# The first product of a two-block kernel in six stages in place of five, and the order of its column groups

## Chip, cores and metric

The kernel runs on one core of a Trainium2 chip. The metric is the device time of one execution in microseconds (us), as the median of several. In the rows below PE is TensorE (PEld its weight loads), DVE VectorE, ACT ScalarE, POOL GpSimd, SP SyncE, which issues most of the DMAs; "Lnnn" is a line of the kernel before.

## What is computed

One sequence of 256 tokens of width 2048 goes through three layers; the change touches only the beginning of the first. Cut to that:

```python
cond = silu(c)
mod = cond @ ada_w[0] + ada_b[0]             # ada_w[0]: 2048 x 6144
shift, scale, gate = split(mod, 3)
h = rms_norm(x, pre_g[0]) * (1 + scale) + shift
u, v, z = split(h @ w_in, 3)                 # w_in: 2048 x 12288
v = layer_norm(gelu(v), norm_g)              # gelu(u), silu(z) and w_out follow
...
x = x + gate * rms_norm(y, post_g[0])
```

All of it is float32. Each product is made of rounded float32r operands: both factors are split into a high part and a rest, and three of the four partial products are added up.

## The kernel before

Everything streams from HBM through two rings of buffers: `raw`, six buffers of 512 KB, for weights and for the rows of `ada_w` that VectorE works on, and five slots of 1 MB (the `s` tiles 7 to 11) for the rows of `ada_w` that TensorE works on. `plan` (L457) writes down in what order the entries are loaded; `fill` (L178) issues them on SP in that order, with at most three entries of look-ahead past one whose ring is full. An entry is issued when the instruction that frees its buffer has been emitted, and SP then waits for that instruction.

The first product is v, 2048 input rows by 4096 columns. It can't begin with all rows at once, because the operand h needs shift and scale, which are themselves a product with 32 MB of `ada_w`. So `stages` (L819) works in stages over the input rows. `STAGES` gives their bounds in tiles of 128 rows. In stage s TensorE multiplies the stage's rows of `w_in` with the part of h that is already there, and between those pieces it makes shift and scale for the rows of stage s+1:

- a piece ("w", `product`, L955) is 256 rows by one group of 512 columns: ScalarE casts the 512 KB of `raw` to the high part `wh` (L885), VectorE subtracts for the rest `wl` (L887), and TensorE runs 12 matmuls of 512 columns (L303 to L305), six for each half of the tokens;
- `mod` (L900) runs the products with `ada_w` (L912), two entries of 1 MB at a time; `rows` (L920) copies their sum out, and `fin` (L927) turns it into columns (L934), adds the bias (L937, L940) and makes the operand's tiles, two at a time, with `h_tiles` (L609: L615 on VectorE, L616 on ScalarE, L620 on VectorE).

There are eight column groups, visited in the order of `ORDER`. Groups 6 and 7 (`STAY`) keep their sums in four PSUM banks through all stages. The other six share three banks, taken in turn by one half of the tokens at a time: at the end of each stage the sum of such a half is copied out by ScalarE (first stage, L970) or added by VectorE to a partial sum in SBUF (L972, tiles `s`, `y`, `wst`), and the bank is free for the half that comes three later. In the last stage the sums go on to a gelu on ScalarE (L765). The eighth bank (7) is that of `mod` and `fin`.

`ahead` (L868) splits weights up to three pieces ahead of the one that TensorE works on, so on VectorE the split of piece p+3 stands before the sums of piece p. It stops at pieces of a stage whose `fin` has not been emitted. When it comes to an entry of the kind "rest" (rows of `ada_w` for the gate, 512 KB each, two VectorE operations L431/L433), it emits that work too. `fin` calls `ahead` once more between its first and its second pair of operand tiles. In the last stage `biases` (L712) puts ten small loads on SP before the fifth piece.

In `plan` a stage of 8 pieces puts the entries of `mod` among its first 5 pieces, then `rows`, one piece, `fin`, and two pieces; a stage of 16 pieces has 12, `rows`, one, `fin`, three. What is left of `ada_w` is spread over the later products by `mix` (L552), at so many entries for each piece.

Of the kernel before, what the change touches and what calls it, by code (L numbers as in the profile page):

```python
# [63 lines left out]
class Entry:  # L64


    def __init__(self, kind, kt, n, loads, pad=False, key=None):
        self.kind, self.kt, self.n, self.loads, self.pad, self.key = kind, kt, n, loads, pad, key
        self.prep = self.use = self.ring = None


class Kernel:
    def __init__(self, ctx, tc, ins, out):
        self.ctx, self.tc, self.nc = ctx, tc, tc.nc
        self.i, self.out = ins, out
        self.W = 512

        self.RAW, self.LOOK, self.AHEAD = 6, 3, 3

        self.STAGES, self.ORDER, self.STAY = [0, 2, 4, 8, 12, 16], (0, 1, 6, 2, 3, 7, 4, 5), (6, 7)  # L80
        self.g = ctx.enter_context(tc.tile_pool(name="g", bufs=1))
        self.ps = ctx.enter_context(tc.tile_pool(name="ps", bufs=1, space=bass.MemoryType.PSUM))
        self.entries, self.issued, self.prepped, self.nraw = [], 0, 0, {}
        self.halves = {}
        self.ready, self.uses, self.adas = deque(), [], deque()
        self.flying, self.landed = [0] * 8, [0] * 8
        self.lanes = [deque() for _ in range(5)]
        self.nn = self.held = 0
        self.sent = set()
        self.taken = [-1] * 8  # L90
        self.banks([0, 1, 2, 3, 4], [5, 6])
# [376 lines left out]
    def plan(self):  # L468
        i = self.i
        E = self.entries  # L470
# [3 lines left out]
        def put(kind, e=None, **at):  # L474
            if e:
                at["n"] = len(E)
                E.append(e)
            self.walk.append((kind, at))

        for s in range(-1, len(self.STAGES) - 1):  # L480
            pieces = []
            if s >= 0:
                k0, k1 = self.STAGES[s:s + 2]
                for g in self.ORDER:
                    for k in range(k0, k1, 2):
                        pieces.append(("w", self.chunk(("v", g), w_in, k * P, 4096 + g * 512), dict(s=s, g=g, k=k)))
            if s + 2 == len(self.STAGES):
                extra = self.ada(0, 2, 0, None)
                for q, (kind, e, at) in enumerate(pieces):
                    if q == 4:  # L490
                        put("biases")
                    put(kind, e, **at)
                    if q >= 8 and extra:
                        put("rest", extra.pop(0))
                break
            k0, k1 = self.STAGES[s + 1:s + 3]
            n = (k1 - k0) * P
            kt = 2048 // n
            mods = []
            for r in range(0, 16, kt):  # L500
                for part in range(2):
                    e = self.chunk(None, i["ada_w"][0], r * P, part * 2048 + k0 * P, kt, n)
                    e.kind, e.ring = "ada0", [7, 8, 9, 10, 11]
                    mods.append(("mod", e, dict(s=s + 1, part=part, r=r, kt=kt)))
            done = 0
            room = max(1, len(pieces) - (3 if len(pieces) == 8 else 4))
            for q in range(room if pieces else 0):
                put(*pieces[q][:2], **pieces[q][2])
                while done < len(mods) and (done + 0.5) * room < (q + 1) * len(mods):
                    put(*mods[done][:2], **mods[done][2])  # L510
                    done += 1
            for kind, e, at in mods[done:]:
                put(kind, e, **at)
            put("rows", s=s + 1)
            for kind, e, at in pieces[room:room + 1]:
                put(kind, e, **at)
            put("fin", s=s + 1)
            for kind, e, at in pieces[room + 1:]:
                put(kind, e, **at)
        rest = []  # L520
        for s in range(1, 4):
            rest += self.ada(0, 2, s, (lambda: self.gate_done(0)) if s == 3 else None)
        for part in (0, 1):
            for s in range(4):
# [1 line left out]
        main = []  # L526
# [3 lines left out]
            main += self.group(("z", g), w_in, 8192 + g * 512, 16)  # L530
        for g in range(4):
            main += self.group(("sgu_out", g), i["sgu_w_out"][0], g * 512, 32)
        E += self.mix(main, rest, [(64, 0.7), (64, 0.2), (56, 0.58)])
        rest = []
        for s in range(4):
            rest += self.ada(1, 2, s, (lambda: self.gate_done(1)) if s == 3 else None)
        w = i["mla_w_in"][0]
        main = []
# [27 lines left out]
        w = i["w_in_2"][0]  # L566
# [280 lines left out]
    def stages(self, h, uv, v_out):  # L847
# [3 lines left out]
        walk, E = self.walk, self.entries  # L851
        n_st = len(self.STAGES) - 1
        parts, room = {}, [3, 3, 3]
# [13 lines left out]
        st = dict(at=0, ahead=0, turn=0, fin=-1)  # L867
        pair = {}  # L868

        def begin(n):  # L870
            self.fill()
            v = self.nraw.pop(n)
            self.prepped = max(self.prepped, n + 1)
            return v

        def ahead(m, mods=True):

            while st["at"] < len(walk):
                kind, at = walk[st["at"]]
                if kind == "w":  # L880
                    if st["ahead"] >= m or at["s"] > st["fin"]:
                        return
                    v = begin(at["n"])
                    hi = self.t("wh", [P, 1024], F32R, bufs=self.LOOK + 1).rearrange("p (k n) -> p k n", n=512)
                    nc.scalar.copy(hi, v)  # L885
                    lo = self.t("wl", [P, 1024], F32R, bufs=self.LOOK + 1).rearrange("p (k n) -> p k n", n=512)
                    nc.vector.tensor_tensor(out=lo, in0=v, in1=hi.bitcast(F32), op=ALU.subtract)  # L887
                    self.freed(E[at["n"]])
                    split[at["n"]] = hi, lo
                    st["ahead"] += 1  # L890
                elif kind == "mod":
                    if at["s"] > st["fin"] + 1 or not mods:
                        return
                elif kind == "rest":
                    for _ in E[at["n"]].prep(begin(at["n"])):
                        pass
                    self.freed(E[at["n"]])
                st["at"] += 1

        def mod(at):  # L900
# [13 lines left out]
                self.freed(E[m])  # L914

        def rest(at):
            if E[at["n"]].use:
                E[at["n"]].use()

        def rows(at):  # L920
            n = (self.STAGES[at["s"] + 1] - self.STAGES[at["s"]]) * P
            st["sum"] = self.t("ada", [P, 512], bufs=2)[:, 0:n]
            nc.scalar.copy(st["sum"], st["rows"][:, 0:n])
            if at["s"] == 0:
                st["fin"] = 0
                ahead(1, False)

        def fin(at):
            s = at["s"]
            k0, k1 = self.STAGES[s:s + 2]  # L930
            m = k1 - k0
            ps = self.bank(7)
            for b in range(m):
                nc.tensor.matmul(ps[:, 2 * b:2 * b + 2], st["sum"][:, b * P:b * P + P], self.halves2, start=True, stop=True)  # L934
            for part in (1, 0):
                o = part * 16 + k0
                nc.vector.tensor_tensor(out=self.mod[0][:, o:o + m], in0=ps[:, part:2 * m:2], in1=self.adab[0][:, o:o + m], op=ALU.add)  # L937
                if part:
                    a = slice(k0, k1)
                    nc.vector.scalar_tensor_tensor(out=self.a1[0][:, a], in0=self.mod[0][:, 16:32][:, a], scalar=1.0, in1=self.preg[0][:, a], op0=ALU.add, op1=ALU.mult)  # L940
            for j in range(k0, k1, 2):
                self.h_tiles(0, (j, j + 1), self.R0)
                if j == k0:
                    st["fin"] = s
                    ahead(min(3, st["ahead"] + 1), False)

        def product(at):
            s, g, k = at["s"], at["g"], at["k"]
# [27 lines left out]
                    v_out(g)(tt, four(ps))  # L976
            st["ahead"] -= 1

        do = dict(w=product, mod=mod, rows=rows, fin=fin, rest=rest, biases=lambda at: self.biases())
        self.banks([], [7])  # L980
        for p, (kind, at) in enumerate(walk):
            left = sum(1 for q in walk[p:] if q[0] == "w")
            if kind in ("w", "mod", "rest"):
                ahead(4 if kind == "w" else 3)
            if kind == "w" and left <= self.LOOK:
                while sum(1 for x in self.ready if x[0] == "piece") < self.LOOK + 1 - left:
                    self.prep_next()
                self.split_ahead(self.LOOK + 1 - left)
            do[kind](at)
# [809 lines left out]
```

## Time and profile before

| | |
|---|---|
| median of three runs | 2614.23 us (2611.59 to 2617.68) |
| the profiled execution | 2612.92 us, span 2611.0 us |
| TensorE busy | 2537.4 us, 97% of the span |
| VectorE, ScalarE busy | 1819.6 us (70%), 1393.2 us (53%) |
| mean granted TensorE clock | 0.991 |

The profile and the rows are those of one execution. The staged product takes the time from about 28 us to 265 us; before it lie the loads of x and the first products with `ada_w`, and after it the products of u, z and the rest of the three layers.

### The profile page before, as it was taken

How to read it: one execution, taken by the hardware profiler on the slowest of the kernel's cores; microseconds unless marked ns; L12 is line 12 of the kernel's file. 1: busy time of each engine (PE TensorE's matmuls, PEld its weight loads, DVE VectorE, ACT ScalarE, POOL GpSimd, SP SyncE). 2: the span in 40 equal slices, each digit the busy share in tenths (PEclk: the TensorE clock that was granted, in tenths of full speed). 3: DMA queues.
4: the chain of work that ended last, by engine and by line, in shares of the span. 5: the costliest groups of instructions: out<-in, count | busy, mean ns of one | idle time of the engine just before them, and what ended most of it. 6: DMA issues, size and time to landing. Idle time of an engine off the chain costs nothing.

```text
span 2611.0 us, 37191 instructions
## 1 busy us (share of the span) xinstructions
PE 2537.4 (97%) x14044; PEld 2166.7 (83%) x14044; DVE 1819.6 (70%) x2664; ACT 1393.2 (53%) x2116; POOL 3.0 (0%) x16
## 2 busy tenths in 40 slices
PE   7998999999998999998999999999999999999999
PEld 5666888888886888887888888888888888888887
DVE  3556898788876788866777777668665556666665
ACT  4334654455444655656566666555544545555554
POOL 0000000000000000000000000000000000000000
PEclk9999999999999999999999999999999999999999
DMA  9976898666884577654535454555556565565653
GB/s 349 355 265 213 304 319 313 208 216 205 313 282 145 179 234 228 211 170 151 160 127 166 148 161 147 191 193 186 194 187 192 188 192 186 187 193 191 195 194 128
DMA packets 302621, 546.02 MB, mean 209 GB/s; under 512 B 27370, under 2 KB 48618, under 8 KB 302058
## 3 DMA queue, kind: packets, MB, share of 16 engines
q1 hardware_dynamic: 300714, 542.71, 63.2%
q8 instruction: 110, 1.80, 0.3%
q10 hardware_dynamic: 1728, 0.94, 0.1%
q14 instruction: 69, 0.57, 0.1%
HBM read 541.48 MB, written 2.10 MB: 208 GB/s over the span
## 4 chain that ended last, share of the span: by engine, by line
PE 82%; DVE 4%; ACT 2%; DMA 2%; issue 1%; SPq 1%; ACTq 0%; DVEq 0%
PE b L295 39%; PE b L296 20%; PE b L303 6%; PE b L305 5%; PE b L304 5%; DVE wl L244 1%; DMA raw<-in_sgu_w_in 1%; ACT wh L241 1%; SPq L173 1%; DVE ada L433 1%; PE b L815 1%; DMA raw<-in_ada_w 1%; PE b L383 0%; DMA raw<-in_mla_w_ukv 0%; DVE R L390 0%
## 5 line engine op out<-in xcount | busy, mean ns | idle before, releaser
L295 PE MATMUL b<-s,wh 128*128 128x512 f32 x4800 | 1696.6, 396 | 7.6 <-DVE s L1091 5.0
L296 PE MATMUL b<-s,wl 128*128 128x256 f32 x4800 | 1344.3, 280 | 0.5 <-DVE wl L244 0.5
L241 ACT CAST wh<-raw 128x1024 fp32r<-128x1024 f32 (+2 forms) x776 | 800.6, 1039 | 859.3 <-PE b L295 563.9
L244 DVE TENSOR_TENSOR wl<-raw,wh 128x1024 fp32r<-128x1024 f32 (+2 forms) x776 | 924.9, 1210 | 249.2 <-ACT wh L241 246.5
L295 PEld LDWEIGHTS b<-s,wh 128*128 128x128 f32 x4800 | 904.1, 188 | 205.8 <-issue 5.4
L296 PEld LDWEIGHTS b<-s,wl 128*128 128x128 f32 x4800 | 904.2, 188 | 2.0 <-DVE wl L244 0.8
L303 PE MATMUL b<-wh,s 128*128 128x512 f32 x816 | 330.6, 405 | 20.3 <-DVE wst L972 11.5
L305 PE MATMUL b<-wh,s 128*128 128x512 f32 x816 | 324.6, 398 | 0.0
L304 PE MATMUL b<-wl,s 128*128 128x512 f32 x816 | 323.4, 396 | 0.0
L303 PEld LDWEIGHTS b<-wh,s 128*128 128x128 f32 x816 | 155.0, 190 | 69.8 <-DVE wst L972 13.3
L305 PEld LDWEIGHTS b<-wh,s 128*128 128x128 f32 x816 | 154.9, 190 | 39.3
L371 DVE TENSOR_TENSOR s<-s,s 128x1024 fp32r<-128x1024 f32 (+1 forms) x82 | 91.6, 1121 | 134.1 <-ACT s L370 134.1
L304 PEld LDWEIGHTS b<-wl,s 128*128 128x128 f32 x816 | 154.8, 190 | 36.1
L433 DVE SCALAR_TENSOR_TENSOR ada<-raw,cond,ada 128x512 f32<-128x512 f32 x240 | 179.6, 748 | 5.6 <-DMA raw<-in_ada_w 2.2
L316 DVE TENSOR_TENSOR cb<-b,ca 128x256 f32<-128x256 f32 x258 | 108.4, 421 | 107.6 <-ACT ca L310 104.0
L310 ACT COPY ca<-b 128x256 f32<-128x256 f32 x338 | 122.9, 368 | 45.4 <-PE b L296 34.7
L887 DVE TENSOR_TENSOR wl<-raw,wh 128x1024 fp32r<-128x1024 f32 x64 | 78.3, 1225 | 94.1 <-ACT wh L885 91.1
L885 ACT CAST wh<-raw 128x1024 fp32r<-128x1024 f32 x64 | 66.5, 1046 | 98.9 <-PE b L305 57.9
L370 ACT CAST s<-s 128x1024 fp32r<-128x1024 f32 (+1 forms) x82 | 79.0, 964 | 13.3 <-DVE s L1170 7.2
L316 DVE TENSOR_TENSOR s<-b,ca 128x256 f32<-128x256 f32 x72 | 29.7, 420 | 22.9 <-ACT ca L310 22.8
L295 PE MATMUL b<-yat,wh 128*128 128x512 f32 x128 | 44.4, 392 | 0.0
L1747 ACT ACTIVATE s<-s 128x256 f32<-128x256 f32 x64 | 26.9, 420 | 17.2 <-DVE s L1746 15.2
(324 smaller groups left out, 1520.5 us busy)
## 6 DMA issues: line engine op xcount, KB each, us to landing
raw<-in_sgu_w_in SPq DMA_DIRECT2D x192, 512.0 KB
raw<-in_w_in SPq DMA_DIRECT2D x148, 512.0 KB
raw<-in_ada_w SPq DMA_DIRECT2D x128, 512.0 KB
raw<-in_w_up SPq DMA_DIRECT2D x128, 512.0 KB
raw<-in_w_down SPq DMA_DIRECT2D x128, 512.0 KB
s<-in_ada_w SPq DMA_DIRECT2D x32, 1024.0 KB
raw<-in_sgu_w_out SPq DMA_DIRECT2D x64, 512.0 KB
raw<-in_mla_w_in SPq DMA_DIRECT2D x40, 512.0 KB
```

Source lines behind the costliest of these rows:

```text
L241: self.nc.scalar.copy(h, v[:, k0:k0 + kn, :])
L244: self.nc.vector.tensor_tensor(out=l, in0=v[:, k0:k0 + kn, :], in1=h.bitcast(F32), op=ALU.subtract)
L295: mm(ps[:, 0:512], h[:, kk, wsl], x, start=start, stop=False, skip_group_check=True)
L296: mm(ps[:, 0:256], l[:, kk, wsl], x[:, 0:256], start=False, stop=stop, skip_group_check=True)
L303: mm(ps, x[:, a:a + P], h[:, kk, wsl], start=start, stop=False, skip_group_check=True)
L304: mm(ps, x[:, a:a + P], l[:, kk, wsl], start=False, stop=False, skip_group_check=True)
L305: mm(ps, x[:, 256 + a:256 + a + P], h[:, kk, wsl], start=False, stop=stop, skip_group_check=True)
L310: self.nc.scalar.copy(c, ps[:, 256:512])
L316: self.nc.vector.tensor_tensor(out=o, in0=ps[:, 0:256], in1=c, op=ALU.add)
L370: self.nc.scalar.copy(dst[:, :, 0:256], raw)
L371: self.nc.vector.tensor_tensor(out=dst[:, :, 256:512], in0=raw, in1=dst[:, :, 0:256].bitcast(F32), op=ALU.subtract)
L433: nc.vector.scalar_tensor_tensor(out=acc[0], in0=v[:, k - k0, :], scalar=col, in1=acc[0], op0=ALU.mult, op1=ALU.add)
```

## The change

```diff
-        self.STAGES, self.ORDER, self.STAY = [0, 2, 4, 8, 12, 16], (0, 1, 6, 2, 3, 7, 4, 5), (6, 7)
+        self.STAGES, self.ORDER, self.STAY = [0, 2, 4, 6, 8, 12, 16], (0, 1, 2, 6, 3, 4, 5, 7), (6, 7)
...
             if s + 2 == len(self.STAGES):
-                extra = self.ada(0, 2, 0, None)
+                extra = (self.ada(0, 2, 0, None) + self.ada(0, 2, 1, None))
+                n_extra = 12
                 for q, (kind, e, at) in enumerate(pieces):
...
-                    if q >= 8 and extra:
+                    if q % 5 in (1, 3) and n_extra:
                         put("rest", extra.pop(0))
+                        n_extra -= 1
                 break
...
             put("fin", s=s + 1)
-            for kind, e, at in pieces[room + 1:]:
+            for kind, e, at in pieces[room + 1:room + 2]:
                 put(kind, e, **at)
-        rest = []
-        for s in range(1, 4):
+            if k1 - k0 > 2:
+                put("more", s=s + 1)
+            for kind, e, at in pieces[room + 2:]:
+                put(kind, e, **at)
+        rest = extra
+        for s in range(2, 4):
             rest += self.ada(0, 2, s, (lambda: self.gate_done(0)) if s == 3 else None)
...
-        E += self.mix(main, rest, [(64, 0.7), (64, 0.2), (56, 0.58)])
+        E += self.mix(main, rest, [(64, 0.66), (64, 0.2), (56, 0.63)])
...
-                elif kind == "rest":
-                    for _ in E[at["n"]].prep(begin(at["n"])):
-                        pass
-                    self.freed(E[at["n"]])
                 st["at"] += 1
...
         def rest(at):
+            for _ in E[at["n"]].prep(begin(at["n"])):
+                pass
+            self.freed(E[at["n"]])
             if E[at["n"]].use:
                 E[at["n"]].use()
...
-            for j in range(k0, k1, 2):
-                self.h_tiles(0, (j, j + 1), self.R0)
-                if j == k0:
-                    st["fin"] = s
-                    ahead(min(3, st["ahead"] + 1), False)
+            self.h_tiles(0, (k0, k0 + 1), self.R0)
+            st["fin"] = s
+
+        def more(at):
+            k0 = self.STAGES[at["s"]]
+            self.h_tiles(0, (k0 + 2, k0 + 3), self.R0)
```

The third stage of 512 rows becomes two of 256. In each stage the groups that stay in PSUM are now the fourth and the last, where they were the third and the sixth. `fin` makes the first pair of operand tiles, and `more`, one piece later, the second pair. The last stage has 16 pieces, of which six (q = 1, 3, 6, 8, 11, 13) are followed by an entry of the gate's rows, where before the last eight were; the others move into the products of u, z and the output.

On VectorE at the end of the last stage but one, from the second L937 of `fin` on (`cb` and `s_51` are the operand's tiles, `wl` a split of weights, `wst` a partial sum, whose `b_306` and `b_307` are the two banks of its group). Before:

```order
L937 TENSOR_TENSOR mod_7_74<-b_308_1438,cols_73 128x4
L615 SCALAR_TENSOR_TENSOR cb_1446<-x_94,a_29_124,R_188 128x256
L615 SCALAR_TENSOR_TENSOR cb_1449<-x_94,a_29_124,R_188 128x256
L620 SCALAR_TENSOR_TENSOR s_51_199<-cb_1446,mod_7_74,s_51_199 128x256
L620 SCALAR_TENSOR_TENSOR s_51_199<-cb_1449,mod_7_74,s_51_199 128x256
L615 SCALAR_TENSOR_TENSOR cb_1454<-x_94,a_29_124,R_188 128x256
L615 SCALAR_TENSOR_TENSOR cb_1457<-x_94,a_29_124,R_188 128x256
L620 SCALAR_TENSOR_TENSOR s_51_199<-cb_1454,mod_7_74,s_51_199 128x256
L620 SCALAR_TENSOR_TENSOR s_51_199<-cb_1457,mod_7_74,s_51_199 128x256
L887 TENSOR_TENSOR wl_1464<-raw_1308,wh_1462 128x1024
L972 TENSOR_TENSOR wst_206<-wst_206,b_306_1424 128x512
L972 TENSOR_TENSOR wst_206<-wst_206,b_307_1431 128x512
```

The same place in the changed kernel, whose line numbers are a few higher (L942 for L937, L621, L626 and L893 for L615, L620 and L887, L978 for L972):

```order
L942 TENSOR_TENSOR mod_7_74<-b_325_1505,cols_73 128x4
L621 SCALAR_TENSOR_TENSOR cb_1513<-x_94,a_29_124,R_188 128x256
L621 SCALAR_TENSOR_TENSOR cb_1516<-x_94,a_29_124,R_188 128x256
L626 SCALAR_TENSOR_TENSOR s_51_199<-cb_1513,mod_7_74,s_51_199 128x256
L626 SCALAR_TENSOR_TENSOR s_51_199<-cb_1516,mod_7_74,s_51_199 128x256
L893 TENSOR_TENSOR wl_1523<-raw_1373,wh_1521 128x1024
L978 TENSOR_TENSOR wst_206<-wst_206,b_323_1491 128x512
L978 TENSOR_TENSOR wst_206<-wst_206,b_324_1498 128x512
L621 SCALAR_TENSOR_TENSOR cb_1541<-x_94,a_29_124,R_188 128x256
L621 SCALAR_TENSOR_TENSOR cb_1544<-x_94,a_29_124,R_188 128x256
L626 SCALAR_TENSOR_TENSOR s_51_199<-cb_1541,mod_7_74,s_51_199 128x256
L626 SCALAR_TENSOR_TENSOR s_51_199<-cb_1544,mod_7_74,s_51_199 128x256
```

The sums of the group that is worked on around `fin` stand ahead of the second pair of operand tiles instead of behind it. That group is the seventh of the order (5) now; before it was 4, also the seventh, with group 5 still to come.

On SP in the last stage, around the end of the small loads (the `raw` from `in_sgu_w_in` are pieces, those from `in_ada_w` entries of the gate). Before:

```order
L728 DMA rows_1608<-in_k_norm 1x64 x2
L730 DMA blk_70<-in_shape_consts 128x128
L173 DMA raw_1624<-in_ada_w 128x2x512
L173 DMA raw_1642<-in_sgu_w_in 128x2x512
L173 DMA raw_1647<-in_ada_w 128x2x512
L173 DMA raw_1668<-in_sgu_w_in 128x2x512
```

In the changed kernel:

```order
L734 DMA rows_1680<-in_k_norm 1x64 x2
L736 DMA blk_70<-in_shape_consts 128x128
L173 DMA raw_1696<-in_sgu_w_in 128x2x512
L173 DMA raw_1716<-in_ada_w 128x2x512
L173 DMA raw_1738<-in_sgu_w_in 128x2x512
L173 DMA raw_1754<-in_sgu_w_in 128x2x512
```

The first load behind the small ones is a piece instead of an entry of the gate, and two pieces in four loads become three. The piece at the head is the twelfth of the stage in both kernels.

## Rows read from the trace of the kernel before

**Rows 1.** Stages 2, 4 and the sum of five: length; PE, PEld, DVE, ACT, POOL; clock, DMA, GB/s.

```profile
58.60:97.00 38.40, 33.66 (x171) 21.37 (x170) 21.32 (x31) 11.65 (x16) 0.00 (x0) 0.94 1.03 375
...
156.00:213.80 57.80, 55.54 (x265) 39.22 (x264) 30.92 (x39) 18.88 (x21) 0.00 (x0) 0.97 0.60 200
...
sum 237.64, PE 220.19 PEld 157.76 DVE 133.49 ACT 92.40 POOL 0.00; mean PE 44.04 PEld 31.55 DVE 26.70 ACT 18.48 POOL 0.00
```

**Rows 2.** Waits of PE from 27 to 266 us: us in total, times, longest.

```profile
PE b L303 <- DVE wst L972: 11.5, 4, 3.9
PE b L303 <- DVE s L972: 3.7, 2, 2.9
...
PE b L303 <- ACT s L970: 2.2, 1, 2.2
```

**Rows 3.** Timeline of PE at two waits: start, us, operation, idle before it.

```profile
147.27 0.39 PE L304 MATMUL b<-wl,s 128*128 128x512 f32 x1
147.50 0.40 PE L305 MATMUL b<-wh,s 128*128 128x512 f32 x1
150.17 0.60 PE L303 MATMUL b<-wh,s 128*128 128x512 f32 x1 [2.27 <-DVE wst L972]
...
261.00 0.50 PE L303 MATMUL b<-wh,s 128*128 128x512 f32 x1 [3.05 <-DVE wst L972]
```

**Rows 4.** Stretches behind two waits: length, PE busy, clock, DMA share, GB/s.

```profile
94.29:99.15 4.86, 4.86 (x11) 0.50 1.05 387
150.17:153.92 3.75, 3.75 (x10) 0.54 0.70 187
```

**Rows 5.** Timeline of DVE before the end of the wait of rows 3.

```profile
145.89 0.88 DVE L615 SCALAR_TENSOR_TENSOR cb<-x,a,R 128x256 f32<-128x256 f32 x2
...
148.29 1.23 DVE L887 TENSOR_TENSOR wl<-raw,wh 128x1024 fp32r<-128x1024 f32 x1 [0.45 <-ACT wh L885]
149.43 1.28 DVE L972 TENSOR_TENSOR wst<-wst,b 128x512 f32<-128x512 f32 x2
```

**Rows 6.** Timeline of DVE in the last stage.

```profile
238.69 1.54 DVE L433 SCALAR_TENSOR_TENSOR ada<-raw,cond,ada 128x512 f32<-128x512 f32 x2 [2.21 <-DMA raw<-in_ada_w]
240.14 1.28 DVE L972 TENSOR_TENSOR s<-s,b 128x512 f32<-128x512 f32 x2
...
260.26 1.28 DVE L972 TENSOR_TENSOR wst<-wst,b 128x512 f32<-128x512 f32 x2
```

**Rows 7.** Timeline of SP in the last stage: the first small load, and the load behind them.

```profile
225.44 0.42 SPq L717 DMA_DIRECT2D bs<-in_sgu_b_s  x1
...
234.35 0.40 SPq L173 DMA_DIRECT2D raw<-in_ada_w  x1
```

**Rows 8.** Timeline of PE: the products with ada_w and the columns of `fin`, short and long stage.

```profile
47.98 1.93 PE L912 MATMUL b<-s,bs 128*32 128x256 f32 x32
...
52.75 0.50 PE L934 MATMUL b<-bs,ada 128*128 128x2 f32 x4
...
137.89 1.92 PE L912 MATMUL b<-s,bs 128*32 128x512 f32 x16
...
142.64 0.95 PE L934 MATMUL b<-bs,ada 128*128 128x2 f32 x8
```

**Rows 9.** Timeline of ACT in the first two stages.

```profile
48.85 1.05 ACT L885 CAST wh<-raw 128x1024 fp32r<-128x1024 f32 x1 [2.02 <-DMA raw<-in_sgu_w_in]
...
59.76 1.07 ACT L885 CAST wh<-raw 128x1024 fp32r<-128x1024 f32 x1
66.67 1.05 ACT L885 CAST wh<-raw 128x1024 fp32r<-128x1024 f32 x1 [5.83 <-DMA raw<-in_sgu_w_in]
```

**Rows 10.** Stretches of the early loads: length, clock, DMA share, GB/s.

```profile
28.00:45.00 17.00, 0.91 1.07 367
45.00:60.00 15.00, 1.00 1.05 386
```

**Rows 11.** Stretch of PE behind the staged product, columns as in rows 4.

```profile
320.00:800.00 480.00, 479.97 (x2830) 1.00 0.79 266
```

More of the change, by code (lines that the diff above doesn't have):

```diff
@@ L977, in product @@
             st["ahead"] -= 1
-        do = dict(w=product, mod=mod, rows=rows, fin=fin, rest=rest, biases=lambda at: self.biases())
+        do = dict(w=product, mod=mod, rows=rows, fin=fin, more=more, rest=rest, biases=lambda at: self.biases())
         self.banks([], [7])
```

## The prediction

> **What bounds the kernel.** TensorE is busy 97% of the span, so I first asked in which stretch the rest is lost. Behind the staged product TensorE does not stop: 479.97 of 480 us are busy from 320 to 800 [rows 11]. In the five stages it is busy 220.2 of 237.6 us [rows 1]. The view of waits gives the idle part there: 11.5 + 3.7 + 2.2 = 17.4 us in seven waits, all before the first matmul on a PSUM bank (L303), six of them for VectorE's addition of an earlier sum out of that bank (L972) and one for ScalarE's copy (L970) [rows 2].
>
> Two more losses hang on them. Idle is counted from the modelled end of a matmul, 0.40 after its start, while the next one starts 0.23 later [rows 3]: each wait costs 0.17 more, 1.2 for seven. And behind three of the waits, those near 94, 150 and 208 us, the granted clock is 0.50 to 0.54, the lower of the two levels, 1.2 GHz [rows 4] (the third stretch, from 208.15 to 211.90, reads like the second). There 11, 9 and 9 matmuls (the shorter stretch counts the next one, which starts on its edge) take 4.86 + 3.75 + 3.75 = 12.36 us; at 0.233 each 29 take 6.76. That is 5.6 us. **All in all 17.4 + 1.2 + 5.6 = 24.2 us** can be had, no more.
>
> Why the banks are late differs by place. At the boundaries (150 us stands for 94 and 208 too) the addition that TensorE waits for starts at 149.43. Ahead of it on VectorE stand the second pair of operand tiles, from 145.89, and a split of weights at 148.29 that waited for a cast, which ScalarE does behind its part of those tiles [rows 5]. In the last stage the addition at 240.14 stands behind a gate entry whose load landed at 238.69; that load was issued at 234.35, behind ten small ones begun at 225.44 [rows 6, 7]. The addition at 260.26, for which TensorE waited 3.05 until 261.00 [rows 3], is behind eight pieces that each brought VectorE a split (1.23), a gate entry (1.54) and, for three groups in four, additions [rows 5, 6]: 1.23 + 1.54 + 0.5 = 3.3 us against 12 x 0.233 = 2.8 us of TensorE. In the first stage the copy stands behind the cast of a piece that has not landed.
>
> **The change part by part.**
>
> *Order of the groups, and the second pair later.* Three banks turn, so a half sum must be out when the third half behind it begins. Before, group 4's first half had to be out when the second half of group 5's first piece began, and `fin` with all its operand tiles lay in between. Now the group behind `fin` is one that stays and takes no bank. Group 5's two halves may wait until the next stage: with two halves of the staying group's piece in between (four in the long stages) there are at least 2.8 us more. On VectorE its additions come after one pair and one or two splits, and ahead of the second pair. Reckoned from the end of the L934 matmuls (in rows 3, 18 matmuls of 0.233 before the wait, so 147.73 - 4.2 = 143.5): the first pair is done when the second begins at 145.89 [rows 5], at about 2.5; two casts and splits until 5.5, addition until 6.1; the bank is wanted at 2 x 2.8 + 1.4 = 7.0. The second pair is wanted one piece into the next stage, at 8.4 in the tightest case, and done at about 8.2 to 8.7. So all three boundary waits go, with their clock: of the waits 11.5 less the last stage's 3.05, call it 8.5, plus 3 x 0.17 plus 5.6, is **14.6 us**. The fifth boundary, which is new, has the same slack. Bound: nothing to the whole if some split is late.
>
> *Four stages of 256 rows.* TensorE's work stays: 64 pieces, and 14 products with `ada_w` of 1.93 or 1.92 us, since 32 matmuls of 256 columns take as long as 16 of 512 [rows 8]; the L934 matmuls go with the rows and are as many. There are 12 more additions of 0.64 on VectorE, 7.7 us. They are hidden: in a short stage VectorE has 8 splits (9.8), 12 additions (7.7) and 2.5 for `fin`, 20 us beside at least 26.7 us of TensorE (22.4 + 2 x 1.95 + 0.4 for L934 [rows 8]), and it is busy 21.3 of 38.4 us now [rows 1]. Without that cover they would cost their 7.7.
>
> *Loads.* The same bytes in another order. Second stage before: 4 MB of pieces and 8 MB of `ada_w` beside 31.0 us of TensorE (22.4 + 4 x 1.95 + 0.8), with DMA at 1.03 of its share, and it took 38.4 [rows 1]. Now the second and third stages load 8.4 million bytes each in 26.7 us, 314 GB/s, under the 386 that the rows show [rows 10]. The fourth has the old second's 12.6 million bytes in 31.0 us, 406 GB/s: too fast by 0.6 million, which the two stages before it have put by, since both rings together hold over 8 million. So from 80 us on no piece is late. The wait that the old second stage had in its middle (3.7 less 2.9, so 0.8 [rows 2], and 0.17) goes: **1.0 us**.
>
> Before that, DMA still leads. First stage: the fifth group visited now begins its second bank half at 27.9 + 1.4 (slow clock at the start, kept) + 6.5 pieces, that is 5 x 2.8 + 2 x 1.95 + 1.4 = 48.6. Its bank is copied out behind the cast of the eighth piece, 48.85 to 49.9 [rows 9], and half a us of copy: 50.4. It waits 1.7, where 2.2 + 0.17 were lost: **0.7 us** gained. Second stage: its fourth piece stands behind as many bytes as before, cast at 59.76 [rows 9], but more of them are narrow rows; 28 to 45 us, with such rows, ran at 367, and 45 to 60 at 386 [rows 10], so 5.6 million bytes come 0.8 later: 60.6. Cast, split and addition end at 63.6, and the bank is wanted 4.2 after the stage's start at 57.8, at 62.0: **a new wait of 1.6 us**. Its bounds are nothing and 5.8, the longest wait of a cast for its load [rows 9].
>
> The Trainium skill, *DMA: Bandwidth & Descriptors*, Specifications, speaks against this part: it gives HBM a limit of about 358 GB/s for a core. By that the fourth stage's loads would take 35.2 us and not 31.0, and if nothing were put by the sum would come out 4.2 us higher. The trace shows 386 over 15 us, so the rows decide.
>
> *Last stage.* Six gate entries in place of eight, spread over 14 pieces, and each emitted at its place instead of three pieces early. VectorE now has 19.7 of splits, 9.2 of gate and 7.7 of additions, 36.6 us beside 44.8. The wait at 261 (3.05 + 0.17) goes. The one at 240.9 (2.91 + 0.17) shrinks. The small loads still hold SP from 11.6 to 20.5 us after the stage's start, and the twelfth piece now goes first behind them; by the 4.3 us that the old first load took [rows 6, 7] it lands at 24.8, and the thirteenth, two loads of 1.4 later, at 27.5. Its split stands ahead of the fourth group's additions: 27.5 + 1.05 + 1.25 + 0.65 = 30.4, wanted at 29.4. **Gain 3.2 + 3.1 - 1.0 = 5.3 us**; bounds 0 and 6.3.
>
> *Later products.* 0.66 entries for a piece in place of 0.7 in u, 0.63 for 0.58 in the output product; TensorE was full there, and two more gate entries are 3 us of VectorE spread over 184 pieces. Nothing; if their cover failed, 3 us.
>
> **Sum.** 14.6 + 1.0 + 0.7 - 1.6 + 5.3 = 20.0 us. The profiled execution took 2612.9 (span 2611.0 and 1.9 around it): 2592.9. The median shown is 1.3 above that execution, so I forecast 2594.2.
>
> **The rivals.**
> - *Starved in the fourth stage.* If the rings don't put by enough, because SP reaches only three entries past a full ring, that stage costs what the old second one did, 38.4 for 31.0: 7.4 us more, 2601.6. For it speaks that DMA fell to 200 GB/s at 156 to 214, with buffers full and entries stuck; against it, that no piece was late for its load there [rows 1].
> - *The last stage keeps its waits.* If the small loads hold SP longer, the stage gains nothing: 2594.2 + 5.3 = 2599.5. For it: the order of the small loads is untouched; against it: the wait at 261 was VectorE's own.
> - *Slower: a bank wait at every boundary.* Group 5's additions now stand behind splits of the next stage's pieces. If the second such piece lands more than 0.9 us after its cast could begin, TensorE stops on the second half of the next stage's first piece; five boundaries at the worst price seen, 3.9 + 0.17 + 2.3 = 6.4, are 32 us: 2626. The rate of 314 GB/s speaks against it, and the waits of casts for loads before 80 us [rows 9] for it at the first two.
> - *No change.* The waits may only move to the next bank, since three banks still turn: 2614.
>
> **Chances.** Forecast 0.73; starved 0.10; last stage 0.10; no change 0.04; slower 0.03. Low end: all 24.2 gone and a run like the fastest, 2.6 below the median: 2587. High end: both starved and no gain in the last stage, 2607. That holds over 0.8 of the cases and the bounds of the new waits. A measurement can tell about 0.2% from no change, 5.2 us, so faster means below 2609: the first three cases, 0.93, less a little for their tails: 0.91, same 0.05, slower 0.04.
>
> **What would show it.** In the new profile the waits of PE for L978 (L972's new line) fall from 15.2 to about 3 us, none of them at the five boundaries, and the clock stays at its upper level from 31 us on. The staged product ends near 245 us instead of 265. Left are a wait of 1 to 2 us near 49 and one near 62, and one about 29 us into the last stage. The prediction is wrong if waits at boundaries remain, if casts wait for loads between 85 and 200 us, or if TensorE stops in the product of u for what moved there.

## The result, and the profile after

| | before | changed |
|---|---|---|
| median, same chip | 2612.91 us (2611.5 to 2617.68, 4 runs) | 2596.12 us (2594.59 to 2597.12, 4 runs) |
| profiled span | 2611.0 | 2594.0 |
| mean granted TensorE clock | 0.991 | 0.994 |
| staged product, first L303 to first L295 | 27.86 to 265.65: 237.8 | 28.14 to 249.04: 220.9 |

The ratio is 0.9932, with an interval from 0.9915 to 0.9949: 16.8 us less, where 20.0 were forecast. The forecast of 2594.2 is 1.9 below the median. Behind the staged product both executions take the same time, 2345.3 and 2345.0 us, so all of the gain was made inside it and none was given back.

Stretches of the changed kernel, with the columns of [rows 1]: the staged product, the stretch with its two last boundaries, and the one behind its longest wait:

```profile
28.14:249.04 220.90, 215.43 (x1116) 157.10 (x1117) 139.35 (x184) 92.75 (x129) 0.00 (x0) 0.99 0.90 310
145.00:215.00 70.00, 69.57 (x330) 50.30 (x330) 44.84 (x59) 30.43 (x39) 0.00 (x0) 1.00 0.80 274
231.99:236.00 4.01, 4.01 (x11) 3.16 (x12) 2.14 (x3) 3.29 (x6) 0.00 (x0) 0.57 0.75 269
```

TensorE is idle for 5.5 of 220.9 us, where it was idle for 17.4 of 237.6. Its waits from 27 to 260 us, to be read beside [rows 2] (the one for L622 lies before the first piece and is there in both kernels):

```profile
PE b L303 <- DVE y L978: 3.0, 1, 3.0
PE b L303 <- ACT s L622: 2.9, 1, 2.9
PE b L303 <- ACT y L976: 1.2, 1, 1.2
PE b L303 <- DVE s L978: 1.2, 2, 0.9
```

The seven waits have become four, and none is at a boundary. More than half of what is left is a single wait in the last stage. The timeline of PE shows it, with the slow clock behind it (compare [rows 3, 4]):

```profile
231.99 0.49 PE L303 MATMUL b<-wh,s 128*128 128x512 f32 x1 [2.95 <-DVE y L978]
232.32 0.43 PE L304 MATMUL b<-wl,s 128*128 128x512 f32 x1
232.55 0.62 PE L305 MATMUL b<-wh,s 128*128 128x512 f32 x1
232.98 0.63 PE L303 MATMUL b<-wh,s 128*128 128x512 f32 x1
...
235.96 0.40 PE L304 MATMUL b<-wl,s 128*128 128x512 f32 x1
```

Eight matmuls from 232.55 start 0.43 apart and not 0.23, at 1.2 GHz. From start to start the last stage lost 4.7 us: 3.1 in the wait, 1.6 by the clock. What the wait hangs on is read backwards, first on DVE, then on ACT, then on SP ([rows 6, 9, 7] are their counterparts):

```profile
228.55 1.53 DVE L433 SCALAR_TENSOR_TENSOR ada<-raw,cond,ada 128x512 f32<-128x512 f32 x2
230.11 1.22 DVE L893 TENSOR_TENSOR wl<-raw,wh 128x1024 fp32r<-128x1024 f32 x1
231.25 1.28 DVE L978 TENSOR_TENSOR y<-y,b 128x512 f32<-128x512 f32 x2
```

```profile
226.32 1.05 ACT L891 CAST wh<-raw 128x1024 fp32r<-128x1024 f32 x1 [3.57 <-DMA raw<-in_sgu_w_in]
229.03 1.04 ACT L891 CAST wh<-raw 128x1024 fp32r<-128x1024 f32 x1 [1.66 <-DMA raw<-in_sgu_w_in]
```

```profile
213.55 0.42 SPq L723 DMA_DIRECT2D bs<-in_sgu_b_s  x1
...
217.10 1.54 SPq L734 DMA_DIRECT2D rows<-in_q_norm  x2
221.04 0.52 SPq L734 DMA_DIRECT2D rows<-in_k_norm  x2
221.61 0.36 SPq L736 DMA_DIRECT2D blk<-in_shape_consts  x1
222.07 0.40 SPq L173 DMA_DIRECT2D raw<-in_sgu_w_in  x1
```

The addition at 231.25 stands behind the split at 230.11, which starts when the cast from 229.03 ends, and that cast waited for a load. The gate entry at 228.55 ends as the cast ends, so it delays nothing. The late loads were issued from 222.07 on, when SP had got through the small ones (eleven with `bs` and `blk`). Among those SP waited for loads to land, as its waits from 199 to 222 us say (the first two lines, for buffers, lie ahead of the small loads):

```profile
SPq L173 <- DVE wl L893: 10.2, 6, 4.3
SPq L173 <- DVE ada L433: 4.3, 2, 2.3
SPq L734 <- DMA raw<-in_sgu_w_in: 2.5, 2, 1.4
SPq L734 <- DMA bs<-in_sgu_b_s: 2.4, 1, 2.4
```

The DMA engines were not the limit. In their rate from 212 to 232 us, in 40 slices of half a us, they stand nearly still from 219.5 to 222.5:

```profile
GB/s 315 270 352 373 242 193 295 352 385 418 434 414 353 169 117 33 50 0 0 1 1 106 91 111 299 397 389 352 377 406 406 385 410 414 385 401 381 361 381 369
```

### The profile page after: what moved, and what is told of

Same layout as the page of the kernel before. It is cut to its first block, busy times and chain, and to the rows that moved or that the text cites. A ratio compares the mean times of both kernels' runs of the same rounds, so it can differ in the third digit from the quotient of the medians.

```text
span 2594.0 us, 37345 instructions
## 1 busy us (share of the span) xinstructions
PE 2531.2 (98%) x14108; PEld 2165.2 (83%) x14108; DVE 1824.8 (70%) x2679; ACT 1390.2 (54%) x2117; POOL 3.0 (0%) x16
## 4 chain that ended last, share of the span: by engine, by line
PE 90%; DVE 3%; DMA 3%; ACT 2%; issue 1%; SPq 0%; ACTq 0%; DVEq 0%
PE b L295 42%; PE b L296 21%; PE b L303 7%; PE b L305 7%; PE b L304 7%; DMA raw<-in_sgu_w_in 2%; PE b L914 1%; PE b L821 1%; DVE wl L244 0%; DMA s<-in_ada_w 0%; ACT wh L241 0%; PE b L383 0%; SPq L173 0%; DVE R L390 0%; ACT wh L891 0%
## 5 line engine op out<-in xcount | busy, mean ns | idle before, releaser
L295 PE MATMUL b<-s,wh 128*128 128x512 f32 x4800 | 1696.1, 396 | 7.4 <-DVE s L1097 4.9
L295 PEld LDWEIGHTS b<-s,wh 128*128 128x128 f32 x4800 | 904.0, 188 | 205.2 <-issue 5.4
L303 PE MATMUL b<-wh,s 128*128 128x512 f32 x816 | 329.3, 404 | 8.3 <-DVE y L978 3.0
L303 PEld LDWEIGHTS b<-wh,s 128*128 128x128 f32 x816 | 154.0, 189 | 54.3 <-issue 5.4
L893 DVE TENSOR_TENSOR wl<-raw,wh 128x1024 fp32r<-128x1024 f32 x64 | 77.3, 1222 | 72.5 <-ACT wh L891 72.3
L295 PE MATMUL b<-yat,wh 128*128 128x512 f32 x128 | 44.4, 392 | 0.0
```

The lines of the kernel that those rows point to most:

```text
L295: mm(ps[:, 0:512], h[:, kk, wsl], x, start=start, stop=False, skip_group_check=True)
L303: mm(ps, x[:, a:a + P], h[:, kk, wsl], start=start, stop=False, skip_group_check=True)
```

## Experiments

Two questions were open: which part of the change removed the waits, and what makes the one that is left. All runs were timed beside the kernel before; its medians in the three sets were 2612.33, 2612.0 and 2613.85. The time behind the staged product differed by some us between profiled executions (2342.5 to 2348.3 over all of these kernels, 2345 to 2347 for most), so the staged product's own length is the sharper number. It differs too: two executions of the changed kernel took 220.9 and 222.0 us for it (the second is e10's), two of the kernel of e6 216.4 and 215.3 (e11). So a difference of about 1 us between single profiles proves nothing.

| run | median us | ratio to before, interval | staged product us |
|---|---|---|---|
| e5_order_alone | 2601.17 | 0.9957 [0.9943, 0.9972] | 225.7 |
| e1_old_order | 2601.74 | 0.9959 [0.9945, 0.9973] | 224.1 |
| e2_pairs_together | 2599.07 | 0.9947 [0.9932, 0.9962] | 223.0 |
| e3_old_stages | 2598.39 | 0.9947 [0.9932, 0.9962] | 223.1 |
| e4_old_gate | 2598.37 | 0.9947 [0.9930, 0.9963] | 222.4 |
| e6_small_on_pool | 2591.78 | 0.9921 [0.9906, 0.9935] | 216.4 |
| e7_no_gate_last | 2592.88 | 0.9924 [0.9909, 0.9939] | 216.1 |
| e8_pool_no_gate | 2594.30 | 0.9930 [0.9915, 0.9945] | 216.8 |
| e9_before_pool | 2611.87 | 0.9991 [0.9982, 1.0000] | 231.3 |
| e10_change_again | 2597.54 | 0.9927 [0.9914, 0.9940] | 222.0 |
| e11_pool_again | 2591.98 | 0.9908 [0.9895, 0.9922] | 215.3 |

**The order alone (e5_order_alone).** The kernel before, with one line of the change:

```diff
-... (0, 1, 6, 2, 3, 7, 4, 5), (6, 7)
+... (0, 1, 2, 6, 3, 4, 5, 7), (6, 7)
```

> The kernel before with the new order of groups alone; stages, pairs and gate weights are as before. Theory: the order removes the three boundary waits with the slow clock behind them, 14.6 us by the sum of the prediction, and leaves the last stage's 6 us of waits: 10 to 15 us faster than before, about 2600, the staged product from 237.8 us to some 223 to 228. Rival (the later second pair is needed too, since VectorE makes it ahead of the sums at the boundary): waits of 2 to 4 us stay at the boundaries of 512 rows, and no more than 6 us are gained, about 2607 to 2611.

11.2 us of the 16.8 are there, and 12.1 of the staged product's 16.9. PE's waits from 27 to 267 us, in this kernel's lines:

```profile
...
PE b L303 <- DVE y L972: 2.8, 1, 2.8
PE b L303 <- DVE s L972: 2.5, 1, 2.5
PE b L303 <- DVE wst L972: 1.9, 2, 1.1
...
```

Of the boundary waits one of 1.15 is left, near 96; none is left near 150 or 208, though both pairs of the operand are made in one go here. And the last stage has a wait of 0.8 near 243 where before lost 3.05 [rows 3], with the gate entries handled as before. So for that wait, too, the order alone is enough. The one of 2.5 at 69.77, in the second stage, was 0.8 before. The rival falls.

**The order undone (e1_old_order).** The reverse of that line, in the changed kernel.

> The changed kernel with one thing undone: the order of the groups in a stage is again 0 1 6 2 3 7 4 5, so that a stage ends on two rotating groups. Theory: the order is what removes the waits for banks at the boundaries. At each of the five boundaries the first group then wants a bank that the fifth group has just filled, and TensorE waits some 1 to 4 us for VectorE's sums; the time goes up by 4 to 14 us, about 2604, the staged product from 220.9 us to some 225 to 235, with the last stage as it is in the changed kernel. Rival: the smaller stages and the second pair made later are what frees VectorE in time, and the order alone is worth under 2 us: 2595 to 2598.

```profile
PE b L303 <- DVE wst L978: 7.6, 6, 1.7
...
```

The waits of the six groups' banks are back: 1.5 to 1.7 at each of the four places from 86 to 153 us, 0.4 near 202. Before, three such waits were 3.94, 2.27 and 2.26 long, with slow matmuls behind each; here no slow matmuls follow. By the reckoning of the prediction the boundaries cost 6.7 + 5 x 0.17 = 7.5 us in place of 14.6. So the theory holds, but the rest of the change takes off about half without the order, the slow clock with it: this kernel is 10.6 us faster than the one before. Undoing the order costs 5.6 us (3.2 of the staged product), not the 11.2 that it gives alone, so the gains of the parts overlap.

What the theory had not foreseen is the last stage: from 198 us on TensorE lost 2.1 us from start to start, in place of 4.7, and the wait in the stage's middle is not there, although the small loads end later here (at 229.34, and the stage begins 6.9 later). In the new order three groups that rotate (3, 4, 5) follow each other just where the late pieces are; in the old one a group that stays, whose bank is its own, stands among them. That is read from the order and was not tried apart.

At the stage's end the old order's wait is 0.94 here, where before lost 3.05. VectorE's work ahead of the addition for which TensorE waits is shown first as it was before (the addition is the one at 260.26 in [rows 6]), then in e1, with its wait on PE:

```profile
251.37 1.23 DVE L887 TENSOR_TENSOR wl<-raw,wh 128x1024 fp32r<-128x1024 f32 x1 [1.75 <-ACT wh L885]
252.51 1.53 DVE L433 SCALAR_TENSOR_TENSOR ada<-raw,cond,ada 128x512 f32<-128x512 f32 x2
...
255.09 1.53 DVE L433 SCALAR_TENSOR_TENSOR ada<-raw,cond,ada 128x512 f32<-128x512 f32 x2
...
257.68 1.53 DVE L433 SCALAR_TENSOR_TENSOR ada<-raw,cond,ada 128x512 f32<-128x512 f32 x2
259.13 1.22 DVE L244 TENSOR_TENSOR wl<-raw,wh 128x1024 fp32r<-128x1024 f32 x1
```

```profile
241.64 2.36 DVE L893 TENSOR_TENSOR wl<-raw,wh 128x1024 fp32r<-128x1024 f32 x2 [1.75 <-ACT wh L891]
243.92 1.53 DVE L433 SCALAR_TENSOR_TENSOR ada<-raw,cond,ada 128x512 f32<-128x512 f32 x2
...
246.50 1.22 DVE L244 TENSOR_TENSOR wl<-raw,wh 128x1024 fp32r<-128x1024 f32 x1
247.64 1.27 DVE L978 TENSOR_TENSOR wst<-wst,b 128x512 f32<-128x512 f32 x2
```

```profile
248.37 0.50 PE L303 MATMUL b<-wh,s 128*128 128x512 f32 x1 [0.94 <-DVE wst L978]
```

Four splits and three gate entries ran back to back before, 8.9 us; here it is four splits and one entry, 6.0 us. Read from these rows, the new places of the gate entries take most of that wait off by themselves, as the order does in e5.

**The pairs together (e2_pairs_together).**

```diff
-            if k1 - k0 > 2:
-                put("more", s=s + 1)
...
-            self.h_tiles(0, (k0, k0 + 1), self.R0)
-            st["fin"] = s
+            for j in range(k0, k1, 2):
+                self.h_tiles(0, (j, j + 1), self.R0)
+                if j == k0:
+                    st["fin"] = s
+                    ahead(min(3, st["ahead"] + 1), False)
```

> The changed kernel with one thing undone: in the two stages of 512 rows the operand's second pair is made right behind the first again, with the splitting step between the two as in the kernel before. Theory: with groups that stay at the fourth and last place, VectorE has the time of a whole group at each boundary, so this is worth 0 to 3 us: 2596 to 2599, with at most one short wait of TensorE at each of the last two boundaries (near 150 and 199). Rival: the second pair delays the sums as it did before, and waits of 2 to 4 us each, with a slow clock behind them, come back at these two boundaries: 6 to 12 us slower, 2602 to 2608.

```profile
PE b L303 <- DVE y L979: 3.5, 1, 3.5
...
PE b L303 <- DVE wst L979: 1.1, 1, 1.1
PE b L303 <- DVE s L979: 0.8, 1, 0.8
```

One boundary wait of 1.1 comes back, at 147.35; the other boundary stays clear. The rival's 6 to 12 us do not come. The staged product is 2.1 longer, of which 1.3 stand at that boundary (1.15 and 0.17); the rest is in the last stage, whose wait also differs from one execution of the changed kernel to the next (e10).

**Five stages (e3_old_stages).** `STAGES` is `[0, 2, 4, 8, 12, 16]` again.

> The changed kernel with one thing undone: the stages are five again, 256, 256, 512, 512 and 512 rows. Theory: the split of a 512-row stage is worth little by itself (the prediction put it at 1.0 less 1.6 us for the wait near 62, a small loss): between 2 us faster and 4 us slower, 2594 to 2600; casts that wait for loads in the second stage may grow, since the conditioning rows of 512 columns must come during a stage of 16 pieces. Rival: the 256-row stages are what keeps the boundaries free, and 5 to 10 us come back near 94 to 150: 2601 to 2606.

```profile
PE b L303 <- DVE y L978: 3.9, 1, 3.9
...
PE b L303 <- DVE s L978: 2.5, 1, 2.5
...
```

No boundary wait returns. The wait in the second stage is at 69.83 and 2.45 long in place of 0.89. The staged product is 2.2 us longer. Of that 1.6 stand at this wait, for loads that come late, and none at a boundary; the rest is no more than two executions of one kernel differ by. The median agrees (2.3 more), but the two intervals overlap, so a gain of the sixth stage is likely and not shown.

**The gate's chunks as before (e4_old_gate).** Eight, one behind each piece from the ninth on, taken up by `ahead`; of the edit one line is shown, and the branch for "rest" in `ahead`, the number of entries and the weights of `mix` go back with it:

```diff
...
-                    if q % 5 in (1, 3) and n_extra:
+                    if q >= 8 and n_extra:
...
```

> The changed kernel with the gate's chunks handled as in the kernel before: eight, one behind each piece from the ninth on, added up during the splitting of weights. The prediction put the gain of the last stage (5.3 us) down to the new handling: then 1 to 5 us come back, 2597 to 2601, as waits of 2 to 3 us near 232 and near the stage's end. Rival (the groups' order alone took away the wait at the end of the last stage, since the stage now ends on a group that stays, and the small loads make the other one whatever the gate does): the time stays at 2595 to 2597, with one wait of about 3 us near 232.

```profile
PE b L303 <- DVE y L979: 3.4, 1, 3.4
...
PE b L303 <- DVE s L979: 1.3, 2, 1.0
```

One wait of 3.37 near 232, none at the stage's end: for the waits the rival is right. The wait is 0.4 longer than in the changed kernel's profile, but in e10 the changed kernel's own wait was 4.33, so no gain of the new handling is shown with the new order. The last stage lost 6.3, 1.6 more than in the changed kernel's first profile and about as much as in e10; 1.2 of the 1.6 are slow matmuls behind the wait, 12 of them start 0.43 apart and not 8. The time fell into the theory's span, and not by its mechanism.

**The small loads on another queue (e6_small_on_pool).** In `biases` each `nc.sync.dma_start` becomes:

```diff
-        nc.sync.dma_start(...)
+        nc.gpsimd.dma_start(...)
```

> The changed kernel with the eleven small loads in the last stage (bs, rows, blk) issued from GpSimd's queue in place of SyncE's. Theory: SyncE stands from 213.6 to 222.1 us in these small loads, the loads of the last stage's later pieces wait behind them, and that is the wait of 2.95 us at 231.99 with the slow clock behind it. Then both go, the staged product shrinks from 220.9 to 216 to 218 us, and the time by 3 to 5 us, about 2592. Rival (the landing buffers that the gate entries hold, or the gate entry on VectorE between the splits of two pieces, are what is late): the wait stays at 2 to 3 us, and the time is 2595 to 2597.

PE's waits, and SP where the small loads stood:

```profile
...
PE b L303 <- DVE s L978: 1.3, 2, 1.1
PE b L303 <- ACT y L976: 1.2, 1, 1.2
```

```profile
210.77 4.53 SPq L173 DMA_DIRECT2D raw<-in_sgu_w_in  x3
216.37 0.37 SPq L173 DMA_DIRECT2D raw<-in_ada_w  x1
220.53 1.82 SPq L173 DMA_DIRECT2D raw<-in_sgu_w_in  x2
```

The wait of the last stage is gone with its slow clock; from start to start that stage loses nothing. The staged product is 4.5 shorter, the median 4.3.

**No gate entries in the last stage (e7_no_gate_last).**

```diff
-                n_extra = 12
+                n_extra = 0
...
-        E += self.mix(main, rest, [(64, 0.66), (64, 0.2), (56, 0.63)])
+        E += self.mix(main, rest, [(64, 0.75), (64, 0.2), (56, 0.63)])
```

> The changed kernel with no gate entries in the last stage: all of them lie among the u groups, whose weight in the merging goes up to take them. If gate entries in the landing buffers are needed for the wait near 232 us (each takes a buffer that a piece would have, so that a piece is loaded fewer pieces ahead), the wait falls below 1 us although the small loads stay on SyncE, and the staged product takes 216 to 218 us; the u groups may pay up to 2 us for more gate entries: 2592 to 2596. If the small loads alone decide, a wait of 2 to 4 us stays and the time is 2595 to 2597.

```profile
210.89 0.42 SPq L723 DMA_DIRECT2D bs<-in_sgu_b_s  x1
...
220.25 5.08 SPq L173 DMA_DIRECT2D raw<-in_sgu_w_in  x5
```

The wait is gone here as well (the stage loses nothing from start to start), though the small loads hold SP for 9.4 us, longer than in the changed kernel. They begin 2.7 earlier, because SP no longer waits for gate entries to leave their buffers, and all six buffers hold pieces, so that the gap is bridged. The edit also takes the entries' work off VectorE in this stage; that this work did not make the wait is read from the rows of the result, where the entry at 228.55 ends as the cast ends, and was not tried apart. In the new order the wait needs both causes, the small loads on SP and the gate entries, and either one taken away is enough.

**Both (e8_pool_no_gate).** The two edits together.

> Both at once: the small loads on GpSimd's queue, and no gate entries in the last stage. If either of the two alone removes the wait near 232 us, this has no more to win than the better of them: 2591 to 2594. If each carries half of it, the whole 4.7 us goes only here.

2594.3: nothing beyond either alone, as the last stage had nothing left to lose. It is 1.4 and 2.5 us above the two, just past the span that was expected.

**The kernel before with its small loads elsewhere (e9_before_pool).** The same edit of `biases`, in the kernel before.

> The kernel before, with nothing changed but the eleven small loads of the last stage, which GpSimd's queue issues. Theory: of the two waits of the last stage of before, the one that ends at 240.88 (2.91 us) is made by the small loads on SyncE and goes, and the one that ends at 261.00 (3.05) is made by the old order, whose last two groups both need a bank, and stays. 2 to 4 us faster than before, about 2609. Rival (both are made by the splits, gate entries and additions on VectorE): both stay, 2611 to 2613. Second rival (both hang on late loads): both go, 5 to 7 us, about 2606.

PE's waits from 27 to 270 us, to be laid beside [rows 2]:

```profile
PE b L303 <- DVE wst L972: 11.5, 4, 3.9
...
PE b L303 <- DVE s L972: 1.3, 2, 0.7
...
```

The wait of 2.91 shrinks to 0.61 and the one of 3.05 stays, so the small loads make the first and not the second, and both rivals fall as they stand. What makes the second this run does not tell: e5 and e1 each take most of it away. Of the time 2.0 us come off, the least that was expected, and the interval reaches up to no change. The staged product is 6.5 shorter, but 2.3 of it is that wait; another 2.0 is the first stage's wait, 0.26 for 2.22 after a start that was 1.7 later, and the rest is a difference of the clock, below. Behind the staged product 2.9 us come back (2348.3 for 2345.3), more than for any other kernel here; where they come from was not followed.

**The changed kernel and the better one on one chip (e10_change_again, e11_pool_again).**

> The changed kernel as it is, to stand beside the other two on one chip: 2594 to 2597.

> The changed kernel with the small loads on GpSimd's queue once more, beside the changed kernel on one chip: 3 to 5 us below it, 2591 to 2593, if the wait near 232 and the slow clock behind it are worth their 4.7 us in the whole time; the same to 1 us if the product of u gives them back.

2597.54 and 2591.98: moving the small loads is worth 5.6 us here. The version beats both kernels, at 0.9908 of the time before.

In e10 the small loads hold SP from 213.26 to 222.96, 9.7 us where it was 8.5 in the first profile of the same kernel, and the wait in the last stage is longer:

```profile
233.07 0.79 PE L303 MATMUL b<-wh,s 128*128 128x512 f32 x1 [4.33 <-DVE y L978]
```

That stage lost 6.1 us here and 4.7 there. In e11, as in e6, it lost nothing.

## Why the prediction was right, and the step that was off

- **The boundaries, 14.6 us: right.** No wait is left at any of five, and none of the slow clock. The order alone leaves one short wait of 1.15 and no slow clock (e5); all the rest without it leaves 7.5 us (e1); making the second pair later adds about 1.3 (e2). The 5.6 us of slow clock in the term hold for one execution: in e9, whose program is the same up to the last stage, the same reckoning gives some 3.3.
- **The second stage's middle, 1.0, and the first stage, 0.7: right.** The first stage's wait is 1.19 + 0.17 where 1.7 were forecast, which makes its gain 1.0.
- **The new wait near 62, 1.6 us lost: right,** with 0.89 + 0.17 = 1.1. The cast it hangs on started at 60.31; the forecast had 60.6.
- **"From 80 us on no piece is late": wrong, at a small price.** Four casts between 85 and 200 us waited 19.2 us in all for their loads, which the prediction had named as a sign of being wrong. Three of them, the longest 7.49 at 124.63, lie in the stage where the first rival saw the loads starve; TensorE had its products with `ada_w` in between, was busy for 31.00 of 31.00 us from 107 to 138, and went through the stage in 31.5 us. The fourth, a cast at 157.16 that waited 5.67, stands ahead of the stop at 160.12 that nobody forecast: 0.28 and 0.17, so 0.45 are given back. The rule in the Trainium skill, DMA: Bandwidth & Descriptors, Specifications, of about 358 GB/s for a core, by which the fourth stage would have cost 4.2 us more, is not borne out: the row of DMA rates above has 0.5 us slices of up to 434 GB/s, [rows 10] 386 over 15 us. The Trainium skill, Perfetto Trace Analysis, Roofline, says that a core alone can go above that share, up to some 435, and there the trace agrees.
- **The last stage, 5.3 us: the step that was off.** 6.3 were lost before and 4.7 now, so 1.6 were gained. The step was the sentence "The small loads still hold SP from 11.6 to 20.5 us after the stage's start". They held it for 8.5 us, about as long as forecast, but from 14.1 to 22.6 (the stage began at 199.47): ahead of them SP now waited 4.3 us for buffers of gate entries, which VectorE frees at their place and no longer three pieces early. With the old handling they begin 11.4 us after the stage's start, and so they do with no entries (e4 at 211.06, e7 at 210.89). The thirteenth piece was cast 29.6 after the start in place of 27.5, and the rest of the chain followed as it was worked out, 2.1 later. To this came 1.6 of slow clock, for which the sum had nothing. In e10 the stage lost 6.1, so there all but about 0.2 of this gain is missing.
- **The cause given for the wait at 261 was one of two.** The prediction blamed VectorE's splits, gate entries and additions, and gave the gain to the gate entries' new places. e1 agrees: with the old order the wait is 0.94, and two entries fewer stand ahead of the addition. But e5 has the old entries and 0.8 by the order alone, whose last two groups no longer both want a bank, and e9 keeps the wait with the small loads gone. So it took both, the order and the entries, and either change would have brought most of the 3.2. e1 has smaller stages as well; that the entries made the difference there is read from VectorE's rows.

By places that is 14.6 - 0.45 + 1.0 + 1.0 - 1.1 + 1.6 = 16.7 us; the staged product shrank by 16.9 and the median by 16.8. Of the rivals, the one in which the small loads hold SP longer came nearest: it was real, at 3.7 of its 5.3 us, and at nearly all of them in e10.

## What to carry to other kernels

When banks or buffers turn among some groups while others keep theirs, put a group that keeps its own wherever the engine that frees them is busy with something else; here that one line gave 11.2 of the 16.8 us alone. But gains of parts that relieve the same engine overlap (the rest alone gave 10.6), so undo each part as well as trying it alone. Small loads that are issued on the queue of the weight stream stop the stream for as long as they wait: here that cost 4.3 to 5.6 us, and nothing where all buffers held weights (e7, e8). Putting them on an idle queue took it away. And when a change moves work that frees a buffer, follow the queue that waits for this buffer up to the next thing behind it, before a time of the old trace is used again.

## What the hardware showed beyond that

The slow clock behind a wait is not a fixed price. In the kernel before it followed the waits of 2.27 and 2.26 us at 150 and 208, but not those of 2.91 and 3.05 in the last stage. In e9 the wait at 149.20 is of 2.26 us, at the same place of a program that is the same up to there, and the clock stays up; behind the next, at 205.64, it drops for a shorter time:

```profile
149.20:152.95 3.75, 3.75 (x16) 3.06 (x17) 2.59 (x3) 1.05 (x1) 0.00 (x0) 1.00 0.69 180
205.64:209.39 3.75, 3.75 (x11) 2.97 (x12) 2.30 (x3) 1.05 (x1) 1.52 (x3) 0.66 0.71 177
```

In [rows 4] the stretch of the same length from 150.17 has 0.54. So one wait costs up to 1.5 us more in one execution than in another. The Trainium skill, TensorE: Matmul & The Clock Gate, Part 1, says that the number of matmuls at the lower level varies from run to run of the same kernel, and speaks of a kernel's start. Behind the waits here the trace shows the like: behind the 3.94 us at 94, 10 matmuls start 0.42 or 0.43 apart in the kernel before and 7 in e9, and behind the next wait 8 and none. What decides it no run here shows.

The other thing is the queue. SP did not only take 0.25 to 0.5 us for each small load: among them it waited for earlier loads to land (4.9 us in three waits, above), and the DMA engines ran empty meanwhile. Why a small load waits for a load of weights was not tried.
